# Rotary and convolution on the projections' banks, decays behind the rotary, and TensorE's side steps tied to products

## The chip, the cores and the metric

One core of a Trainium2 chip runs the whole program in one launch. The metric is the device time of that launch in microseconds (us). TensorE is PE (its weight load PEld), VectorE DVE, ScalarE ACT, GpSimd POOL; SyncE (SP) issues most loads.

## The reference, cut to what matters

Two layers of an encoder on 256 rows of 1024. Each layer projects the normalised rows, runs retention, a gated recurrence (LRU) and grouped-query attention on parts of the projection, adds the output projection, and then an expert stage (PEER). In float32:

```python
for l in range(DEPTH):                                   # 2
    h = rms_norm(x, ln1_w[l])
    rq, rk, rv, rg, lx, lgt, aq, ak, av = split_cols(h @ w_in[l], widths)
    o_ret = retention_group(rq, rk, rv, rg, ret_log_decay[l], ...)
    o_lru = rglru_group(lx, lgt, lru_conv_w[l], lru_conv_b[l], lru_gate_w[l], ...)
    o_att = attention_group(aq, ak, av, attn_q_norm[l], attn_k_norm[l], ax_cos, ax_sin)
    x = x + concat([o_ret, o_lru, o_att]) @ w_out[l]
    x = x + peer(rms_norm(x, ln2_w[l]), ...)
return rms_norm(x, lnf_w)

# attention: q, k normalised per head of 64, then rotary
qh = qh * cos + axial_rotate_half(qh) * sin              # the same for kh
o = softmax(qh @ kh.T * scale) @ vh
# LRU: 4-tap convolution along the rows (2 to the left, 1 to the right), two gates per direction, scan
xc = conv(xb, conv_w) + conv_b
# retention: scores times exp(log_decay * |i - j|)
scores = (q @ k.T) * dmat
```

## The kernel before, in words

Every product of two float32 matrices is made of three products of a high and a low half (`three`, L210). `split` (L144) makes the halves: ACT rounds `raw` to `hi`, and DVE or POOL subtracts to get `lo`. Weights arrive by SP in tiles `raw` (a ring of 4), `hi` and `lo` are rings of 4 as well, and nearly all splits of the mixing stage have their low half on POOL.

The mixing stage (`mix`, L249) runs once per layer, in these steps:

- Norm and transposes of the rows, in two blocks of 128 (`norm_rows` L175, `norm_T` L196).
- The attention's projection (`matt` L317): sums in three PSUM banks of the ring `acc` (4 banks), two for q and one for k and v of both blocks. Banks are copied to `qk` and `vt` (L344 to L346).
- The convolution's projection (L447 to L459): 4 weight tiles of 24 products each into both banks of the ring `hd`, called `pl`. `pl[0]` is copied into the padded tile `xpad` (L462), `pl[1]` into `gb`.
- The retention's projection (L529 to L540): 8 weight tiles of 12 products each into all four `acc` banks.
- The output projection (L611 on), then the expert stage (`peer`).

Beside the products runs side work, written as generators and advanced by a queue `Side` (L88): after a weight tile, `side.adv(us)` lets as many steps through as the given us pay for. The steps: `att` (L351: squares, `srq` = the power of the norm on POOL, rotary into `ro`, k scaled into `k2`, transposes to `qT` and `kT`; then scores, exponentials and the weighted sum), `lru` (L465: convolution, gates, scan), `decays` (L293: the retention's `dec`) and later `ret`. In layer 0 `setup` (L222) makes constants of the LRU by a chain of tiny DVE instructions.

What order instructions have on an engine is set by a scheduler that takes the ready instruction by its own estimates; `tc.issue_after(i)` adds the edge that what is written inside stands behind `i` on its engine. Each engine then runs its list in order. The scores take two `hd` banks at a time, `pe`; the gates take `hd` banks too.

Of the kernel before, what the change touches and what calls it, by code (L numbers as in the profile page):

```python
# [9 lines left out]
F32 = mybir.dt.float32  # L10
# [3 lines left out]
AF = mybir.ActivationFunctionType  # L14
# [4 lines left out]
P = 128  # L19
# [95 lines left out]
def trunk(ctx, tc, x, rows, lru_col, lru_gw, w_in, w_out, ln2_w, peer_wq, peer_kt, peer_ut, peer_v, lnf_w,  # L115
# [56 lines left out]
            st.enter_context(tc.issue_after(i))  # L172
        return st

    def norm_rows(wrow, tt, xn, add=None):  # L175

        st = sp.tile([P, 3], F32, tag="nst", bufs=4, name="nst")
        sq = sp.tile([P, 512], F16, tag="junk", bufs=1, name="junk")
        hs = [slice(hf * 512, (hf + 1) * 512) for hf in range(2)]
        for hf, o in enumerate(hs):  # L180
            if add is not None:
                V.tensor_add(xs[:, tt, o], xs[:, tt, o], add[hf])
            A.activation(sq, xs[:, tt, o], AF.Square, scale=1.0 / 32, accum_out=st[:, hf:hf + 1])
        with tc.issue_after(seen[0]) if tt else ExitStack():
            V.tensor_mul(xn[:, hs[0]], xs[:, tt, hs[0]], wrow[:, hs[0]])
        sm = V.tensor_scalar(st[:, 2:3], st[:, 0:1], st[:, 1:2], EPS, op0=ADD, op1=ADD)
        rs = sp.tile([P, 1], F32, tag="nrs", bufs=4, name="nrs")
        mark(G.tensor_tensor(rs, st[:, 2:3], mhalf[:, :1], op=POW))
        seen[0] = sm.ins
        with tc.issue_after(sm.ins):  # L190
            V.tensor_mul(xn[:, hs[1]], xs[:, tt, hs[1]], wrow[:, hs[1]])
        for o in hs:
            V.tensor_scalar(xn[:, o], xn[:, o], rs, None, op0=MUL)
            yield o

    def norm_T(wb, hiT, loT, tt, add=None, xn=None):  # L196
        if xn is None:
            xn = raw_tile()
        for o in norm_rows(wb, tt, xn, add):
            pt = tr_tile()  # L200
            for k in range(4):
                c = o.start + k * P
                TE.transpose(pt[:, k * P:(k + 1) * P], xn[:, c:c + P], ident)
            pv = pt.rearrange("p (k t) -> p k t", k=4)
            c = o.start // P
            o3 = (slice(None), slice(c, c + 4), slice(tt * P, (tt + 1) * P))
            mark(A.activation(hiT[o3], pv, AF.Copy))
            mark(V.tensor_sub(loT[o3], pv, hiT[o3].bitcast(F32)))

    def three(o, lh, ll, rh, rl, first, last, skip=False):  # L210
        TE.matmul(o, lh, rh, start=first, stop=False, skip_group_check=skip)  # L211
        TE.matmul(o, lh, rl, start=False, stop=False, skip_group_check=skip)  # L212
        TE.matmul(o, ll, rh, start=False, stop=last, skip_group_check=skip)  # L213

    hT = cp.tile([P, ND, T], F32R, name="hT")
    lT = cp.tile([P, ND, T], F32R, name="lT")
# [32 lines left out]
    def mix(l, mp, ms):  # L249
# [43 lines left out]
        def decays():  # L293
            V.tensor_scalar(gnw, gnw, 0.5, None, op0=MUL)

            for h in range(RH):
                tmp = ms.tile([P, NT, T], F32, tag="dtmp", bufs=1, name="dtmp")
                fw, bw = lg[:, h:h + 1], lg[:, RH + h:RH + h + 1]
                V.tensor_scalar(tmp, mnt[:, 1], bw, None, op0=MUL)
                V.scalar_tensor_tensor(tmp, mnt[:, 0], fw, tmp, op0=MUL, op1=ADD)  # L300
                A.activation(dec[:, h], tmp, AF.Exp)
                yield 1.2
# [34 lines left out]
        for d in range(HL, ND):  # L337
            watt(d)
            for tt in range(NT):
                matt(d, tt)  # L340
        qk = mp.tile([P, NT, 10, HD], F32, name="qk")
        vt = mp.tile([P, NT, P], F32, name="vt")
        for tt in range(NT):
            A.activation(qk[:, tt, 0:8], pq[tt].rearrange("p (h e) -> p h e", e=HD), AF.Copy)  # L344
            A.activation(qk[:, tt, 8:10], pkv[:, tt * T:tt * T + 128].rearrange("p (h e) -> p h e", e=HD), AF.Copy)
            V.tensor_copy(vt[:, tt], pkv[:, tt * T + 128:(tt + 1) * T])  # L346
        qT = mp.tile([P, 4, T], F32, name="qT")
        kT = mp.tile([P, 2, T], F32, name="kT")
        srq = mp.tile([P, NT, 10], F32, name="srq")

        def att():  # L351
            for tt in range(NT):
                sqt = ms.tile([P, 10, HD], F32, tag="art", name="asq")
                A.activation(sqt, qk[:, tt], AF.Square)
                ss = ms.tile([P, 10], F32, tag="ass", name="ass")
                V.tensor_reduce(ss, sqt, axis=AX.X, op=ADD)
                V.tensor_scalar(ss, ss, 1.0 / HD, EPS, op0=MUL, op1=ADD)
                G.tensor_tensor(srq[:, tt], ss, mhalf[:, :10], op=POW)
                ro = ms.tile([P, 10, HD], F32, tag="aro", name="aro")
                rt = ms.tile([P, 10, HD], F32, tag="art", name="art")  # L360
                for a, b, w in ((0, 8, 0), (8, 10, 1)):
                    V.tensor_mul(ro[:, a:b], qk[:, tt, a:b],
                                 acw[:, tt, w].unsqueeze(1).to_broadcast([P, b - a, HD]))
                    x5 = qk[:, tt, a:b].rearrange("p h (r s e) -> p h r s e", r=2, s=2)
                    r5 = rt[:, a:b].rearrange("p h (r s e) -> p h r s e", r=2, s=2)
                    s5 = asw[:, tt, w].rearrange("p (r s e) -> p r s e", r=2, s=2)
                    for s in range(2):
                        V.tensor_mul(r5[:, :, :, s], x5[:, :, :, 1 - s],
                                     s5[:, :, s].unsqueeze(1).to_broadcast([P, b - a, 2, 16]))
                V.tensor_add(ro, ro, rt)  # L370

                k2 = ms.tile([P, 2, 2, HD], F32, tag="k2", name="k2")
                for g in range(2):
                    A.activation(k2[:, g], ro[:, 8 + g].unsqueeze(1).to_broadcast([P, 2, HD]), AF.Copy,
                                 scale=srq[:, tt, 8 + g:9 + g])
                V.tensor_scalar(srq[:, tt], srq[:, tt], HD ** -0.5, None, op0=MUL)
                t = slice(tt * P, (tt + 1) * P)
                pt = tr_tile()
                for c in range(4):
                    TE.transpose(pt[:, c * P:(c + 1) * P], ro[:, 2 * c:2 * c + 2].rearrange("p h e -> p (h e)"), ident)  # L380
                V.tensor_copy(qT[:, :, t], pt.rearrange("p (c t) -> p c t", c=4))
                pt = tr_tile()
                for c in range(2):
                    TE.transpose(pt[:, c * P:(c + 1) * P], k2[:, c].rearrange("p o e -> p (o e)"), ident)
                A.activation(kT[:, :, t], pt[:, :2 * P].rearrange("p (c t) -> p c t", c=2), AF.Copy)
                yield 5.0
# [23 lines left out]
            for tt in range(NT):  # L410
# [24 lines left out]
                split(pt.rearrange("p (c t) -> p c t", c=4), mixH[:, 4:8, t], mixL[:, 4:8, t])  # L435
                yield 1.2

        side.add(att())
        side.adv(5.0)


        xpad = mp.tile([P, 2, T + 4], F32, name="xpad")
        gb = mp.tile([P, 2, T], F32, name="gb")
        V.memset(xpad, 0.0)
        if l == 0:
            setup()
        pl = [hd_tile() for _ in range(2)]  # L447
        for d2 in range(ND // 2):
# [5 lines left out]
            for k in range(2):  # L454
                d = d2 * 2 + k
                for c in range(4):
                    s = slice(k * 512 + c * P, k * 512 + (c + 1) * P)
                    three(pl[c // 2][:, (c % 2) * T:(c % 2 + 1) * T], hi[:, s], lo[:, s], hT[:, d], lT[:, d],
                          d == 0 and c % 2 == 0, d == ND - 1, skip=True)  # L459
# [70 lines left out]
        for d in range(ND):  # L530
# [4 lines left out]
            for tt in range(NT):  # L535
                t = slice(tt * P, (tt + 1) * P)
                for hf in range(2):
                    o = slice(hf * 512, (hf + 1) * 512)
                    three(pr4[tt][hf], hT[:, d, t], lT[:, d, t], hi[:, o], lo[:, o], d == 0, d == ND - 1)
# [435 lines left out]
```

## Time and profile before

| | |
|---|---|
| median of 3 runs | 1975.03 us (1974.86 to 1975.09) |
| the profiled execution, and its span | 1972.67 us, 1970.9 us |
| busy: PE, PEld | 1881.8 us (95%), 1671.8 us (85%) |
| busy: DVE, ACT, POOL | 1509.9 us (77%), 902.9 us (46%), 553.0 us (28%) |
| loaded | 321.16 MB, 163 GB/s over the span |

Layer 0's mixing stage takes about the first 165 us, layer 1's that from about 985 to 1140 us; the rest is the expert stage. In the page's table of 40 slices PE is at 9 tenths nearly everywhere else, and at 5 to 8 in these two stretches. PE's share is an average over both kinds of stages, so what a change in the mixing stage is worth has to be read there.

### The profile page before, as it was taken

How to read it: one execution, taken by the hardware profiler on the slowest of the kernel's cores; microseconds unless marked ns; L12 is line 12 of the kernel's file. 1: busy time of each engine (PE TensorE's matmuls, PEld its weight loads, DVE VectorE, ACT ScalarE, POOL GpSimd, SP SyncE). 2: the span in 40 equal slices, each digit the busy share in tenths (PEclk: the TensorE clock that was granted, in tenths of full speed). 3: DMA queues.
4: the chain of work that ended last, by engine and by line, in shares of the span. 5: the costliest groups of instructions: out<-in, count | busy, mean ns of one | idle time of the engine just before them, and what ended most of it. 6: DMA issues, size and time to landing. Idle time of an engine off the chain costs nothing.

```text
span 1970.9 us, 34224 instructions
## 1 busy us (share of the span) xinstructions
PE 1881.8 (95%) x13452; PEld 1671.8 (85%) x13452; DVE 1509.9 (77%) x2660; ACT 902.9 (46%) x1384; POOL 553.0 (28%) x240
## 2 busy tenths in 40 slices
PE   5888999999999999999978889999999999999998
PEld 5678999999999877788866689999999998777886
DVE  7676999789855699755576669996997557996555
ACT  4544444444444443444445344445444444334443
POOL 5425888200000132100073268881000002330000
PEclk9899999999999999999988999999999999999999
DMA  6225555544455544555552255555445555446553
GB/s 210 81 66 190 162 183 187 190 159 161 162 187 186 172 144 157 185 189 190 168 160 75 70 198 172 184 188 188 151 160 171 191 183 170 140 151 201 185 190 129
DMA packets 95138, 324.43 MB, mean 165 GB/s; under 512 B 10112, under 2 KB 10624, under 8 KB 94720
## 3 DMA queue, kind: packets, MB, share of 16 engines
q1 hardware_dynamic: 92672, 315.66, 48.8%
q10 hardware_dynamic: 2304, 6.59, 1.0%
q8 instruction: 105, 1.72, 0.4%
q14 instruction: 57, 0.47, 0.1%
HBM read 321.16 MB, written 1.05 MB: 163 GB/s over the span
## 4 chain that ended last, share of the span: by engine, by line
PE 77%; DVE 13%; issue 4%; POOL 3%; ACT 1%; DMA 1%; POOLq 0%; SPq 0%; DVEq 0%; ACTq 0%
PE acc L212 12%; PE acc L213 12%; PE acc L211 12%; PE hd L211 6%; PE hd L212 6%; PE hd L213 6%; PE tr L211 6%; PE tr L212 6%; PE tr L213 6%; DVE ob L791 2%; POOL lo L146 2%; DVE oa L794 2%; DVE Gt L806 1%; DVE pl L146 1%; DVE lo L146 1%
## 5 line engine op out<-in xcount | busy, mean ns | idle before, releaser
L145 ACT ACTIVATE hi<-raw 128x1024 fp32r<-128x1024 f32 (+1 forms) x600 | 627.9, 1047 | 507.1 <-issue 176.8
L146 POOL TENSOR_TENSOR lo<-raw,hi 128x1024 fp32r<-128x1024 f32 (+1 forms) x206 | 527.0, 2564 | 1175.0 <-ACT hi L145 1134.9
L146 DVE TENSOR_TENSOR lo<-raw,hi 128x1024 fp32r<-128x1024 f32 (+1 forms) x394 | 485.2, 1233 | 197.2 <-ACT hi L145 197.2
L211 PE MATMUL acc<-hi,ph 128*128 128x512 f32 x1024 | 410.7, 401 | 0.0
L213 PE MATMUL acc<-hi,pl 128*128 128x512 f32 x1024 | 405.3, 396 | 0.4 <-DVE pl L146 0.4
L212 PE MATMUL acc<-lo,ph 128*128 128x512 f32 x1024 | 405.4, 396 | 0.0
L211 PE MATMUL hd<-hT,hi 128*128 128x256 f32 x1088 | 311.2, 286 | 0.6 <-ACT hi L145 0.6
L213 PE MATMUL hd<-hT,lo 128*128 128x256 f32 x1088 | 308.3, 283 | 2.2 <-POOL lo L146 2.2
L212 PE MATMUL hd<-lT,hi 128*128 128x256 f32 x1088 | 308.0, 283 | 0.0
L211 PE MATMUL tr<-hT,hi 128*128 128x256 f32 x1024 | 291.2, 284 | 0.0
L145 ACT ACTIVATE ph<-Gt 128x256 fp32r<-128x256 f32 x256 | 106.4, 417 | 401.9 <-PE acc L212 392.1
L212 PE MATMUL tr<-lT,hi 128*128 128x256 f32 x1024 | 288.1, 281 | 0.0
L213 PE MATMUL tr<-hT,lo 128*128 128x256 f32 x1024 | 287.9, 281 | 0.0
L213 PEld LDWEIGHTS acc<-hi,pl 128*128 128x128 f32 x1024 | 192.9, 188 | 47.3 <-DVE pl L146 2.0
L212 PEld LDWEIGHTS acc<-lo,ph 128*128 128x128 f32 x1024 | 193.3, 189 | 41.1
L211 PEld LDWEIGHTS acc<-hi,ph 128*128 128x128 f32 x1024 | 193.1, 189 | 40.8 <-ACT ph L145 0.5
L146 DVE TENSOR_TENSOR pl<-Gt,ph 128x256 fp32r<-128x256 f32 x256 | 123.2, 483 | 126.9 <-ACT ph L145 126.9
L213 PEld LDWEIGHTS hd<-hT,lo 128*128 128x128 f32 x1088 | 207.3, 191 | 2.6 <-POOL lo L146 2.6
L211 PEld LDWEIGHTS hd<-hT,hi 128*128 128x128 f32 x1088 | 207.6, 191 | 2.2 <-ACT hi L145 0.8
L212 PEld LDWEIGHTS hd<-lT,hi 128*128 128x128 f32 x1088 | 207.3, 191 | 0.9
L211 PEld LDWEIGHTS tr<-hT,hi 128*128 128x128 f32 x1024 | 193.4, 189 | 1.1
L212 PEld LDWEIGHTS tr<-lT,hi 128*128 128x128 f32 x1024 | 193.3, 189 | 1.0
(206 smaller groups left out, 2536.5 us busy)
## 6 DMA issues: line engine op xcount, KB each, us to landing
raw<-in_peer_ut_dram SPq DMA_DIRECT2D x256, 512.0 KB, 3.4
raw<-in_peer_v_dram SPq DMA_DIRECT2D x256, 512.0 KB, 3.6
raw<-in_peer_wq_dram SPq DMA_DIRECT2D x32, 512.0 KB, 4.2
raw<-in_w_in_dram SPq DMA_DIRECT2D x24, 512.0 KB, 3.7
raw<-in_w_out_dram SPq DMA_DIRECT2D x16, 512.0 KB, 3.4
raw<-in_w_in_dram SPq DMA_DIRECT2D x16, 384.0 KB, 4.0
Gt<-in_peer_kt_dram ACTq DMA_DIRECT2D x2, 1024.0 KB, 4.7
xs<-in_x_dram SPq DMA_DIRECT2D x2, 512.0 KB, 6.0
```

What stands on the lines that cost most here:

```text
L145: A.activation(hi, src, AF.Copy)
L146: (lo_eng or V).tensor_sub(lo, src, hi.bitcast(F32))
L211: TE.matmul(o, lh, rh, start=first, stop=False, skip_group_check=skip)
L212: TE.matmul(o, lh, rl, start=False, stop=False, skip_group_check=skip)
L213: TE.matmul(o, ll, rh, start=False, stop=last, skip_group_check=skip)
L791: V.tensor_tensor(four(ob), iop(0, P), pair(1, P), op=EQ)
L794: V.tensor_mul(four(oa[:, z]), four(oe), pair(2 + z, SW))
L806: V.scalar_tensor_tensor(g, pv[:, o:o + n], 1.0 / GS, g, op0=MUL, op1=MUL)
```

## The change

- `norm_rows` and `norm_T` can give the last scaling of the first half of a row block to ACT; the mixing stage's two norms do so.
- The copies `qk` and `xpad` are gone. Squares, rotary products and convolution read the `acc` and `hd` banks; the convolution's taps are cut at the ends in place of padding. `vt` is copied by ACT.
- `att` makes the rotary of both blocks first, then the transposes of both; `decays` is tied on DVE behind the last rotary sum.
- The gates' products go to a `tr` bank in place of an `hd` bank.
- The side steps during the last two tiles of the convolution's projection, and all during the retention's, are tied behind the last product before them (`side_adv`).

```diff
-    def norm_rows(wrow, tt, xn, add=None):
+    def norm_rows(wrow, tt, xn, add=None, act=False):
...
-        for o in hs:
-            V.tensor_scalar(xn[:, o], xn[:, o], rs, None, op0=MUL)
+        for hf, o in enumerate(hs):
+            if act and hf == 0:
+                A.activation(xn[:, o], xn[:, o], AF.Copy, scale=rs)
+            else:
+                V.tensor_scalar(xn[:, o], xn[:, o], rs, None, op0=MUL)
...
-                V.tensor_scalar(tmp, mnt[:, 1], bw, None, op0=MUL)
+                with tc.issue_after(last[0].ins):
+                    V.tensor_scalar(tmp, mnt[:, 1], bw, None, op0=MUL)
...
-        qk = mp.tile([P, NT, 10, HD], F32, name="qk")
-        for tt in range(NT):
-            A.activation(qk[:, tt, 0:8], pq[tt].rearrange("p (h e) -> p h e", e=HD), AF.Copy)
-            A.activation(qk[:, tt, 8:10], pkv[:, tt * T:tt * T + 128].rearrange("p (h e) -> p h e", e=HD), AF.Copy)
-            V.tensor_copy(vt[:, tt], pkv[:, tt * T + 128:(tt + 1) * T])
...
+                qp = pq[tt].rearrange("p (h e) -> p h e", e=HD)
+                kp = pkv[:, tt * T:tt * T + 128].rearrange("p (h e) -> p h e", e=HD)
-                A.activation(sqt, qk[:, tt], AF.Square)
+                A.activation(sqt[:, 0:8], qp, AF.Square)
+                A.activation(sqt[:, 8:10], kp, AF.Square)
...
-                V.tensor_add(ro, ro, rt)
+                A.activation(vt[:, tt], pkv[:, tt * T + 128:(tt + 1) * T], AF.Copy)
+                last[0] = V.tensor_add(ro, ro, rt)
...
+                turned.append((ro, k2))
+                yield 5.0
+            for tt in range(NT):
+                ro, k2 = turned[tt]
...
         side.add(att())
-        side.adv(5.0)
-        xpad = mp.tile([P, 2, T + 4], F32, name="xpad")
+        side.adv(10.0)
+        def side_adv(us):
+            with tc.issue_after(lastp[0].ins):
+                side.adv(us)
...
-            if d2 == 1:
-                side.adv(5.0)
-        A.activation(xpad[:, :, 2:2 + T], pl[0].rearrange("p (c t) -> p c t", c=2), AF.Copy)
+            if d2 >= 2:
+                side_adv(5.0)
...
-                V.tensor_scalar(xc[:, ct], xpad[:, ct, 0:T], w(0), w(4), op0=MUL, op1=ADD)
-                for j in range(1, 4):
-                    V.scalar_tensor_tensor(xc[:, ct], xpad[:, ct, j:j + T], w(j), xc[:, ct], op0=MUL, op1=ADD)
+                px = pl[0][:, ct * T:(ct + 1) * T]
+                V.tensor_scalar(xc[:, ct], px, w(2), w(4), op0=MUL, op1=ADD)
+                for j, a, b in ((0, 2, T), (1, 1, T), (3, 0, T - 1)):
+                    V.scalar_tensor_tensor(xc[:, ct, a:b], px[:, a + j - 2:b + j - 2], w(j), xc[:, ct, a:b],
+                                           op0=MUL, op1=ADD)
...
-                    pg = hd_tile()
+                    pg = tr_tile()
...
-            side.adv(R_MIX)
+            side_adv(R_MIX)
```

How that moves instructions, at three places of layer 0 (L145 and L146 are `split`; the names are those of the code, and behind the arrow stands what is read).

PE, where the transposes of the rotary's block 0 stand among the products of the convolution's projection. Before:

```order
L213 MATMUL hd<-hT,lo 128x256
L211 MATMUL hd<-hT,hi 128x256
L212 MATMUL hd<-lT,hi 128x256
L380 MATMUL tr<-ident,aro 128x128 x4
L384 MATMUL tr<-ident,k_334 128x128
L213 MATMUL hd<-hT,lo 128x256
L384 MATMUL tr<-ident,k_334 128x128
L211 MATMUL hd<-hT,hi 128x256
```

and after:

```order
L215 MATMUL hd<-hT,hi 128x256
L216 MATMUL hd<-lT,hi 128x256
L217 MATMUL hd<-hT,lo 128x256
L389 MATMUL tr<-ident,aro 128x128 x4
L393 MATMUL tr<-ident,k_329 128x128 x2
L215 MATMUL hd<-hT,hi 128x256
L216 MATMUL hd<-lT,hi 128x256
```

Before, 38 of the 96 products stand ahead of them, after 72; those of block 1 then stand behind all 96 (60 before).

ACT, from the high halves of the attention's last weight tiles (128x768) to the first reads of the `acc` banks. Before:

```order
L235 ACTIVATE lt_358<-lt_357 128x8
L145 ACTIVATE hi<-raw 128x768 x2
L301 ACTIVATE dec<-dtmp 128x512
L145 ACTIVATE hi<-raw 128x768 x2
L301 ACTIVATE dec<-dtmp 128x512
L145 ACTIVATE hi<-raw 128x1024
L301 ACTIVATE dec<-dtmp 128x512
L145 ACTIVATE hi<-raw 128x1024
L301 ACTIVATE dec<-dtmp 128x512
L145 ACTIVATE hi<-raw 128x1024
L344 ACTIVATE qk<-acc 128x512 x2
```

and after:

```order
L145 ACTIVATE hi<-raw 128x768 x3
L239 ACTIVATE lt_362<-lt_361 128x8
L145 ACTIVATE hi<-raw 128x768
L145 ACTIVATE hi<-raw 128x1024 x3
L358 ACTIVATE asq<-acc 128x512
L359 ACTIVATE asq<-acc 128x128
L145 ACTIVATE hi<-raw 128x1024
L358 ACTIVATE asq<-acc 128x512
L374 ACTIVATE vt<-acc 128x128
```

The exponentials of the decays are gone from between the high halves; `setup`'s exponential (`lt`, L235 before, L239 after) has moved behind three of them.

DVE, from the rotary's last sum to the reduces of the first scores. Before:

```order
L370 TENSOR_TENSOR aro<-aro,art 128x640
L381 COPY qT<-tr 128x4x128
L376 TENSOR_SCALAR srq<-srq 128x10
L469 TENSOR_SCALAR xc<-xpad,pcol 128x256 x2
L471 SCALAR_TENSOR_TENSOR xc<-xpad,pcol,xc 128x256 x6
L515 TENSOR_SCALAR gu<-gu 128x512
L516 TENSOR_TENSOR gu<-gu,gb 128x512
L399 TENSOR_REDUCE sm<-hd 128x2 x2
```

and after, the middle of the same stretch:

```order
L390 COPY qT<-tr 128x4x128
L485 SCALAR_TENSOR_TENSOR xc<-hd,pcol,xc 128x254
L485 SCALAR_TENSOR_TENSOR xc<-hd,pcol,xc 128x255
L304 TENSOR_SCALAR dtmp<-mnt,prm 128x512
L485 SCALAR_TENSOR_TENSOR xc<-hd,pcol,xc 128x255
L483 TENSOR_SCALAR xc<-hd,pcol 128x256
L305 SCALAR_TENSOR_TENSOR dtmp<-mnt,prm,dtmp 128x512
L485 SCALAR_TENSOR_TENSOR xc<-hd,pcol,xc 128x254
L408 TENSOR_REDUCE sm<-hd 128x2
L485 SCALAR_TENSOR_TENSOR xc<-hd,pcol,xc 128x255
L410 SCALAR_TENSOR_TENSOR sm<-sm,srq 128x2
```

The decays' instructions (L304, L305) now lie among the convolution's, and the first reduce stands ahead of the convolution's end.

## Rows read from the trace of the kernel before

**Rows 1.** the page's chain that ended last, shares of the span by engine
```profile
PE 77%; DVE 13%; issue 4%; POOL 3%; ACT 1%; DMA 1%; POOLq 0%; SPq 0%; DVEq 0%; ACTq 0%
```

**Rows 2.** PE timeline, layer 0: start, length, line, shapes [idle before, releaser], us
```profile
35.90 0.28 PE L211 MATMUL hd<-hT,hi 128*128 128x256 f32 x1
...
51.06 1.09 PE L380 MATMUL tr<-ident,aro 128*128 128x128 f32 x4 [6.08 <-DVE aro L370]
...
62.26 0.40 PE L211 MATMUL acc<-hi,hT 128*128 128x512 f32 x1
...
94.71 0.60 PE L417 MATMUL tr<-ident,pr 128*128 128x128 f32 x4
```

**Rows 3.** PE timeline, layer 1, the same columns
```profile
1014.12 0.28 PE L211 MATMUL hd<-hT,hi 128*128 128x256 f32 x1
...
1014.24 0.28 PE L212 MATMUL hd<-lT,hi 128*128 128x256 f32 x1
...
1026.27 1.08 PE L380 MATMUL tr<-ident,aro 128*128 128x128 f32 x4 [7.05 <-DVE aro L370]
...
1037.46 0.39 PE L211 MATMUL acc<-hi,hT 128*128 128x512 f32 x1
...
1070.12 0.60 PE L417 MATMUL tr<-ident,pr 128*128 128x128 f32 x4
```

**Rows 4.** POOL timeline, layer 0
```profile
39.50 7.58 POOL L146 TENSOR_TENSOR lo<-raw,hi 128x1024 fp32r<-128x1024 f32 x3 [3.71 <-ACT hi L145]
...
49.91 2.08 POOL L358 TENSOR_TENSOR srq<-ass,mhalf 128x10 f32<-128x10 f32 x1 [2.84 <-DVE ass L357]
...
130.92 2.35 POOL L146 TENSOR_TENSOR lo<-raw,hi 128x1024 fp32r<-128x1024 f32 x1 [4.64 <-ACT hi L145]
```

**Rows 5.** DVE timeline, layer 0
```profile
33.47 2.35 DVE L243 TENSOR_SCALAR lt<-lt 128x8 f32<-128x8 f32 x1
...
35.85 0.17 DVE L242 TENSOR_TENSOR lt<-lt,lt 128x8 f32<-128x8 f32 x1
...
36.05 0.17 DVE L243 TENSOR_SCALAR lt<-lt 128x8 f32<-128x8 f32 x1
...
41.98 5.65 DVE L362 TENSOR_TENSOR aro<-qk,acw 128x512 f32<-128x512 f32 x2 [2.19 <-ACT qk L344]
...
63.48 6.72 DVE L471 SCALAR_TENSOR_TENSOR xc<-xpad,pcol,xc 128x256 f32<-128x256 f32 x6
...
71.18 1.28 DVE L399 TENSOR_REDUCE sm<-hd 128x2 f32<-128x512 f32 x2
...
130.36 1.28 DVE L574 SCALAR_TENSOR_TENSOR dec<-hd,dec 128x512 f32<-128x512 f32 x2
```

**Rows 6.** ACT timeline, layer 0
```profile
37.84 0.63 ACT L301 ACTIVATE dec<-dtmp 128x512 f32<-128x512 f32 x1 [4.53 <-DVE dtmp L300]
...
47.86 0.28 ACT L345 ACTIVATE qk<-acc 128x128 f32<-128x128 f32 x1 [4.38 <-DVE vt L346]
...
74.27 0.56 ACT L405 ACTIVATE pr<-hd,sm,srq 128x256 f32<-128x256 f32 x1
```

**Rows 7.** DVE timeline, layer 1
```profile
988.90 3.97 DVE L193 TENSOR_SCALAR pr<-pr,nrs 128x512 f32<-128x512 f32 x2
...
1000.76 0.48 DVE L299 TENSOR_SCALAR dtmp<-mnt,prm 128x512 f32<-128x512 f32 x1
...
1001.27 0.75 DVE L300 SCALAR_TENSOR_TENSOR dtmp<-mnt,prm,dtmp 128x512 f32<-128x512 f32 x1
```

**Rows 8.** DVE groups by shape, 0 to 165 us: names, shapes, count | busy us, mean ns | idle
```profile
L356 DVE TENSOR_REDUCE ass<-asq 128x10 f32<-128x640 f32 x2 | 1.6, 809 | 0.0
...
L597 DVE TENSOR_TENSOR rsq<-gg,rss 128x256 f32<-128x256 f32 x2 | 0.8, 420 | 0.8 <-POOL rss L594 0.8
...
L596 DVE TENSOR_TENSOR gg<-hd,gg 128x256 f32<-128x256 f32 x2 | 0.8, 417 | 0.0
```

More of the change, by code (lines that the diff above doesn't have):

```diff
@@ L191, in norm_rows @@
             V.tensor_mul(xn[:, hs[1]], xs[:, tt, hs[1]], wrow[:, hs[1]])
-        for o in hs:
-            V.tensor_scalar(xn[:, o], xn[:, o], rs, None, op0=MUL)
+        for hf, o in enumerate(hs):
[3 more added lines that the diff above has]
+                V.tensor_scalar(xn[:, o], xn[:, o], rs, None, op0=MUL)
             yield o
     def norm_T(wb, hiT, loT, tt, add=None, xn=None):
+        act = xn is not None
         if xn is None:
             xn = raw_tile()
-        for o in norm_rows(wb, tt, xn, add):
+        for o in norm_rows(wb, tt, xn, add, act):
             pt = tr_tile()
@@ L212, in three @@
         TE.matmul(o, lh, rl, start=False, stop=False, skip_group_check=skip)
-        TE.matmul(o, ll, rh, start=False, stop=last, skip_group_check=skip)
+        return TE.matmul(o, ll, rh, start=False, stop=last, skip_group_check=skip)
     hT = cp.tile([P, ND, T], F32R, name="hT")
@@ L351, in att @@
         def att():
+            turned = []
             for tt in range(NT):
+                qp = pq[tt].rearrange("p (h e) -> p h e", e=HD)
+                kp = pkv[:, tt * T:tt * T + 128].rearrange("p (h e) -> p h e", e=HD)
                 sqt = ms.tile([P, 10, HD], F32, tag="art", name="asq")
-                A.activation(sqt, qk[:, tt], AF.Square)
+                A.activation(sqt[:, 0:8], qp, AF.Square)
+                A.activation(sqt[:, 8:10], kp, AF.Square)
                 ss = ms.tile([P, 10], F32, tag="ass", name="ass")
@@ L360, in att @@
                 rt = ms.tile([P, 10, HD], F32, tag="art", name="art")
[L361 to L364, printed above, removed]
+                for a, b, w, src in ((0, 8, 0, qp), (8, 10, 1, kp)):
+                    V.tensor_mul(ro[:, a:b], src, acw[:, tt, w].unsqueeze(1).to_broadcast([P, b - a, HD]))
+                    x5 = src.rearrange("p h (r s e) -> p h r s e", r=2, s=2)
                     r5 = rt[:, a:b].rearrange("p h (r s e) -> p h r s e", r=2, s=2)
@@ L436, in att @@
                 yield 1.2
+        last = [None]
         side.add(att())
-        side.adv(5.0)
-        xpad = mp.tile([P, 2, T + 4], F32, name="xpad")
+        side.adv(10.0)
+        def side_adv(us):
+            with tc.issue_after(lastp[0].ins):
+                side.adv(us)
         gb = mp.tile([P, 2, T], F32, name="gb")
-        V.memset(xpad, 0.0)
         if l == 0:
@@ L457, in mix @@
                     s = slice(k * 512 + c * P, k * 512 + (c + 1) * P)
-                    three(pl[c // 2][:, (c % 2) * T:(c % 2 + 1) * T], hi[:, s], lo[:, s], hT[:, d], lT[:, d],
-                          d == 0 and c % 2 == 0, d == ND - 1, skip=True)
-            if d2 == 1:
-                side.adv(5.0)
-        A.activation(xpad[:, :, 2:2 + T], pl[0].rearrange("p (c t) -> p c t", c=2), AF.Copy)
+                    lastp = [three(pl[c // 2][:, (c % 2) * T:(c % 2 + 1) * T], hi[:, s], lo[:, s], hT[:, d], lT[:, d],
+                                   d == 0 and c % 2 == 0, d == ND - 1, skip=True)]
+            if d2 >= 2:
+                side_adv(5.0)
         A.activation(gb, pl[1].rearrange("p (c t) -> p c t", c=2), AF.Copy)
@@ L538, in mix @@
                     o = slice(hf * 512, (hf + 1) * 512)
-                    three(pr4[tt][hf], hT[:, d, t], lT[:, d, t], hi[:, o], lo[:, o], d == 0, d == ND - 1)
-            side.adv(R_MIX)
+                    lastp = [three(pr4[tt][hf], hT[:, d, t], lT[:, d, t], hi[:, o], lo[:, o], d == 0, d == ND - 1)]
+            side_adv(R_MIX)
         rqk = mp.tile([P, NT, 8, HD], F32, name="rqk")
```

## The prediction

> **What bounds the kernel now.** I read the chain of waits on the page first: TensorE (PE) carries 77% of it [rows 1], so only time in which PE stands still can be won. Nearly all of the span is the expert stage, which the change leaves as it is. It touches the mixing stage, run once per layer, and there I followed PE's own list of instructions. In layer 0 the first product of the convolution's projection (96 products into the hd banks) starts at 35.90, the first product of the retention projection at 62.26 and the first transpose of softmax weights at 94.71 [rows 2]; in layer 1 the same marks are 1014.12, 1037.46 and 1070.12 [rows 3]. So 96 products, 0.12 us apart [rows 3] and worth 11.5 us, take 26.4 and 23.3 us. The reader is to see why: PE stands 6.08 us in layer 0 and 7.05 us in layer 1 for aro, the rotary's sum [rows 2, 3].
>
> Behind both stands one thing. A VectorE (DVE) instruction on SBUF data that meets a split on GpSimd (POOL) ends only when the split ends: an eight-column instruction took 2.35 us where its like takes 0.17, and the rotary's first two products 5.65 us, while POOL ran splits back to back from 39.50 to 47.08 [rows 4, 5]. The decays (four times two DVE instructions and an exponential on ScalarE, ACT) sit in front of the rotary. ACT stood 4.53 us for one of them [rows 6] with the next split's high half queued behind it, and so POOL stood 3.71 us [rows 4]. The copies out of the banks wait too: one copy of k stood 4.38 us for DVE's copy of v [rows 6]. DVE on a bank is not held up so: two instructions with a PSUM operand took 1.28 us together beside a split that ran from 130.92 to 133.27 [rows 4, 5].
>
> **The change part by part.** I count per layer against these marks, in the time of the profiled execution, 1972.67 us (its span 1970.9 and 1.8 around it). The median of the runs is 2.4 us above that, which I add at the end.
>
> *Norm.* One half of each normalised row goes to ACT. In layer 1 the two halves on DVE took 3.97 us together behind two splits [rows 7]; the half that stays waits for one split at most and ACT's half for none, so the first transposes come some 2 us sooner: -2. In layer 0 there is no such stretch, and the load of the LRU's parameters now stands behind the norm on ACT's queue. I take -0.5, between 0 and -2.
>
> *From the convolution's projection to the retention products.* Gone are ACT's copies of q and k and its copy into xpad, a memset, and from DVE the copies of v (now ACT's). None is on PE's path once the rotary doesn't wait for them: 0. The square, the rotary's products and the convolution read the banks. That could be dearer per instruction, but the same 128x256 shape takes 417 ns with an operand in a bank and 420 ns from SBUF alone [rows 8]: 0 again. [...]
>
> With the decays gone from the front, ACT gives out high halves as data comes, and POOL's own queue sets the pace: three splits after the one that the first products need, the power for block 0 (srq), one split, the power for block 1. A split is 2.35 us and a power 2.08 [rows 4]: 4 x 2.35 + 2 x 2.08 = 13.6 us after the projection's start. ACT's k2 and two transposes are 1.2 more (k2's like, the exponential, is 0.56 [rows 6]). PE meanwhile does 72 products (8.6 us), block 0's transposes and 24 products (2.9 us), and is not later. 14.8 us in place of 23.3 in layer 1: -8.5.
>
> In layer 0 a chain of 21 tiny DVE instructions, setup(), is ahead of the rotary in DVE's queue. By the order its exponential now comes behind three high halves on ACT, so the chain falls among POOL's splits and gets one instruction through per split: about 8 by the end of the last. Then POOL has nothing before the rotary's sum of squares, and the other 13 go at 0.2 us each [rows 5], 2.6 us. Block 0's rotary as far as srq costs a 128x512 product (0.64), two 128x256 (0.83) and the reduce (0.81) [rows 5, 8], 2.3 us. That puts everything behind the third split 4.9 us later: 14.8 + 4.9 = 19.7 in place of 26.4, -6.7. If the chain passes unhindered it is as in layer 1, 26.4 - 14.8 = 11.6 saved.
>
> *From there to the first transpose of softmax weights.* 48 products lie between these marks, before as after, in 32.5 us. Two things move against each other. Against: DVE had the convolution (its six updates 6.72 us) and gelu before the scores' reduce at 71.18, 8.9 us after the first product [rows 2, 5]. Now the convolution is 8 x 0.42 = 3.4 [rows 8], but the decays, 4 x (0.48 + 0.75) = 4.9 [rows 7], lie among it, and I let four of their instructions meet a split of 2.35 us. The convolution also holds the bank that the second half of the first score group needs, and ACT's copies of k's transposes stand behind the decays' exponentials, so PE waits twice for some 4 us. The second reduce comes some 16 us after the first product: +7. For: the LRU's gates go to the tr banks. Before, they shared the two hd banks with the scores, and from the first score groups' last exponential, 74.83, to 94.71 it took 19.9 us [rows 2, 6]. What ACT has to do in it is twelve exponentials at 0.56 [rows 6] and twelve activations of the gates of the same width, some 13 us: -7. The loss is in the queues and sure; the gain needs everything to fit, so I count 4 of it: +3 per layer, with ends 0 and +7.
>
> *After that* DVE and PE do the same work in nearly the same order: 0.
>
> Sum: layer 0 -0.5 - 6.7 + 3 = -4.2; layer 1 -2 - 8.5 + 3 = -7.5. Together -11.7: 1961.0 in the profiled execution's time, **1963.4 us** as a median.
>
> **Rivals.**
> 1. *Given back behind the decays.* If the gates' own banks win nothing, the third term is +7 in both layers: -0.2 and -3.5, 1971.3 us. For it: the scores were late before, with DVE's queue full [rows 5], and that queue gets fuller. Against it: scores and gates visibly take turns on two banks.
> 2. *Slower: the scores start too late.* One mechanism decides. The eight decay instructions, and the three small ones on SBUF among them, can each end with a split of its own. Four meetings are in the sum; each further one costs 2.35 us, since PE's products are tied behind the scores and can't go ahead. The saving of 11.7 us is used up with 5 further meetings, two and a half per layer. With eight meetings per layer it is 8 x 2.35 - 11.7 = 7 us slower, 1982 us. Against it: ACT's high halves stand behind the decays' exponentials, so POOL runs dry and leaves DVE alone.
> 3. *All of it holds.* The gates' banks bring the whole 7 and the setup chain slips through between the splits: -1.5, -11.6 and 0 in layer 0, -2, -8.5 and 0 in layer 1. That is -23.6, 1951.4 us.
> 4. *The stall is not moved.* The tensor add that ends the rotary still reads SBUF and can wait for a split, and with it PE. If PE's 6.08 and 7.05 us stay, the second terms shrink to about -1 and -1.5, and 1976 us is left, no change that could be told.
>
> **How the numbers follow.** The forecast gets 0.60, case 1 0.15, case 4 0.06, case 2 0.10 and case 3 0.09. A measurement of this kernel can tell about 0.2%, 4 us, from no change. Faster by more than that: the forecast, case 3 and a third of case 1, 0.74. Within 0.2% (1971.1 to 1979.0): the rest of case 1, case 4 and a little of case 2, 0.17. Slower: 0.09. The range reaches from 1951 (case 3) to 1975 (case 1 with one or two more meetings) and leaves out about 0.15.
>
> **What would show it.** PE's wait for aro falls to under 5 us in layer 0 and under 2 in layer 1. The first retention product comes 20 us after the first hd product in layer 0 and 15 in layer 1. Between it and the first softmax transposes PE waits for the scores' inputs twice, some 4 us each, for ACT (gb, k's transposes) and for DVE (the convolution); the rotary's 128x512 product takes some 0.7 us, not 2.8. The second term is wrong if POOL shows gaps between the projection's splits; the third if the softmax transposes come over 37 us or under 31 us after the first retention product.

## The result and the profile after

The changed kernel takes **1961.19 us** (median of 4 runs, 1956.96 to 1963.86) against 1974.94 us of the kernel before in the same comparison: ratio 0.9936, 95% interval 0.9925 to 0.9948. It is faster by 0.64%; 1963.4 us was predicted, with a range of 1951 to 1975. The profiled execution took 1961.07 us, its span is 1959.3.

The page's busy times and its chain that ended last (answers to [rows 1]):

```profile
PE 1879.7 (96%) x13452; PEld 1671.3 (85%) x13452; DVE 1491.7 (76%) x2650; ACT 904.3 (46%) x1386; POOL 565.0 (29%) x240
PE 78%; DVE 16%; issue 3%; ACT 1%; POOL 1%; DMA 1%; POOLq 0%; SPq 0%; DVEq 0%; ACTq 0%
```

TensorE's list in layer 0 (start, length, line, shapes [idle before, releaser]; answers to [rows 2]; line numbers are 4 to 15 higher than before):

```profile
35.39 0.28 PE L215 MATMUL hd<-hT,hi 128*128 128x256 f32 x1
...
48.28 1.09 PE L389 MATMUL tr<-ident,aro 128*128 128x128 f32 x4 [4.21 <-DVE aro L375]
...
57.58 0.67 PE L389 MATMUL tr<-ident,aro 128*128 128x128 f32 x4 [4.24 <-DVE qT L390]
...
58.33 0.78 PE L215 MATMUL acc<-hi,hT 128*128 128x512 f32 x1
...
70.92 1.30 PE L403 MATMUL hd<-kT,qT 64*128 64x256 f32 x4 [4.05 <-DVE xc L485]
...
90.74 0.60 PE L426 MATMUL tr<-ident,pr 128*128 128x128 f32 x4
...
129.26 2.38 PE L600 MATMUL hd<-rv,dec 128*128 128x64 f32 x12 [0.19 <-DVE dec L589]
...
131.97 4.36 PE L600 MATMUL hd<-rv,dec 128*128 128x64 f32 x20
...
138.79 0.63 PE L615 MATMUL tr<-ident,rsq 128*128 128x128 f32 x2
```

And in layer 1 (answers to [rows 3]):

```profile
1011.40 0.28 PE L215 MATMUL hd<-hT,hi 128*128 128x256 f32 x1
...
1019.92 0.60 PE L389 MATMUL tr<-ident,aro 128*128 128x128 f32 x4
...
1027.87 1.11 PE L389 MATMUL tr<-ident,aro 128*128 128x128 f32 x4 [4.14 <-DVE qT L390]
...
1029.06 0.78 PE L215 MATMUL acc<-hi,hT 128*128 128x512 f32 x1
...
1039.92 1.13 PE L403 MATMUL hd<-kT,qT 64*128 64x256 f32 x4 [2.50 <-DVE xc L485]
...
1060.64 0.60 PE L426 MATMUL tr<-ident,pr 128*128 128x128 f32 x4
...
1100.84 2.34 PE L600 MATMUL hd<-rv,dec 128*128 128x64 f32 x20
...
1104.46 0.42 PE L615 MATMUL tr<-ident,rsq 128*128 128x128 f32 x2
```

The wait of 7.05 us for the rotary's sum is gone in layer 1, and that of layer 0 is 4.21 instead of 6.08. In the place of the old waits stand new ones: 4.24 and 4.14 us for the copy `qT`, which must empty a tr bank before block 1 can be transposed, and 4.05 and 2.50 us for the convolution. VectorE's list in layer 0 shows why `qT` is late; GpSimd's power for block 1 and its next split stand above it:

```profile
50.92 2.00 POOL L363 TENSOR_TENSOR srq<-ass,mhalf 128x10 f32<-128x10 f32 x1 [0.18 <-DVE ass L362]
52.85 2.34 POOL L146 TENSOR_TENSOR lo<-raw,hi 128x1024 fp32r<-128x1024 f32 x1
```

```profile
52.92 2.82 DVE L305 SCALAR_TENSOR_TENSOR dtmp<-mnt,prm,dtmp 128x512 f32<-128x512 f32 x1
...
56.44 0.48 DVE L304 TENSOR_SCALAR dtmp<-mnt,prm 128x512 f32<-128x512 f32 x1 [0.62 <-ACT dec L306]
56.84 0.68 DVE L390 COPY qT<-tr 128x512 f32<-128x512 f32 x1
```

A decay instruction (0.75 us where nothing meets it, [rows 7]) ended at 55.74, 0.55 us behind the split that ran from 52.85 to 55.19, and a second decay instruction, which waited for the first one's exponential, stood ahead of the copy.

Layer 0 was 3.97 us ahead at its first softmax transposes (90.74 for 94.71) and 0.48 us *behind* at the retention's (138.79 against 138.31 in the kernel before, the line below). Its waits between these marks are 4.1 us together, 3.9 before.

```profile
138.31 0.42 PE L600 MATMUL tr<-ident,rsq 128*128 128x128 f32 x2
```

But TensorE ran at half its clock there (granted 0.50). The windows view of the stretch, before and then after (busy us of PE, PEld, DVE, ACT and POOL, then the granted clock, DMA share, GB/s):

```profile
130.00:140.00 10.00, 9.06 (x56) 7.13 (x57) 5.49 (x14) 2.85 (x5) 4.36 (x3) 1.00 0.33 104
```

```profile
130.00:140.00 10.00, 10.00 (x39) 9.10 (x39) 3.09 (x9) 2.21 (x4) 2.02 (x2) 0.50 0.00 0
```

The 20 products of line 600 took 4.36 us in layer 0, at half clock, and 2.34 in layer 1, at full clock. At the end of layer 0 the changed kernel is 1.5 us ahead, and layer 1 adds 10.1.

### The profile page after: what moved, and what is told of

Read it like the earlier page. It is cut to its first block, busy times and chain, and to the rows that moved or that the text cites. A ratio compares the mean times of both kernels' runs of the same rounds, so it can differ in the third digit from the quotient of the medians.

```text
span 1959.3 us, 34218 instructions
## 1 busy us (share of the span) xinstructions
PE 1879.7 (96%) x13452; PEld 1671.3 (85%) x13452; DVE 1491.7 (76%) x2650; ACT 904.3 (46%) x1386; POOL 565.0 (29%) x240
## 4 chain that ended last, share of the span: by engine, by line
PE 78%; DVE 16%; issue 3%; ACT 1%; POOL 1%; DMA 1%; POOLq 0%; SPq 0%; DVEq 0%; ACTq 0%
PE acc L216 12%; PE acc L217 12%; PE acc L215 12%; PE hd L215 6%; PE tr L215 6%; PE hd L216 6%; PE hd L217 6%; PE tr L216 6%; PE tr L217 6%; DVE ob L806 2%; DVE oa L809 2%; DVE Gt L821 2%; DVE lo L146 2%; DVE pl L146 2%; PE hd L816 1%
## 5 line engine op out<-in xcount | busy, mean ns | idle before, releaser
L146 POOL TENSOR_TENSOR lo<-raw,hi 128x1024 fp32r<-128x1024 f32 (+1 forms) x206 | 539.9, 2629 | 1151.6 <-ACT hi L145 1112.7
L145 ACT ACTIVATE hi<-raw 128x1024 fp32r<-128x1024 f32 (+1 forms) x600 | 629.9, 1050 | 509.1 <-issue 176.6
L146 DVE TENSOR_TENSOR lo<-raw,hi 128x1024 fp32r<-128x1024 f32 (+1 forms) x394 | 489.9, 1244 | 199.8 <-ACT hi L145 199.5
L145 ACT ACTIVATE ph<-Gt 128x256 fp32r<-128x256 f32 x256 | 106.9, 419 | 400.0 <-PE acc L216 390.8
L146 DVE TENSOR_TENSOR pl<-Gt,ph 128x256 fp32r<-128x256 f32 x256 | 124.9, 490 | 127.0 <-ACT ph L145 127.0
```

Of the source, the lines that this page charges most:

```text
L145: A.activation(hi, src, AF.Copy)
L146: (lo_eng or V).tensor_sub(lo, src, hi.bitcast(F32))
```

## The experiments

Twelve kernels ran, most of them the changed kernel with one edit. "Clock" is the mean granted clock over the timed executions, and it matters: within one kernel (the rotary on SBUF, below) single executions went from 1960.0 us at 0.986 to 1975.4 at 0.976. A least-squares line through all 118 executions, one level per kernel and one common slope, gives 1.26 us (plus or minus 0.16, 95%) per 0.001 of clock. The last column is each kernel's level at 0.983 by that line; it is a reading, not a measurement.

It may take too much away from an edit. In the traces of all these kernels the half clock lies in the mixing stages, where the edits act: 0.87 to 0.97 was granted there (0 to 165 and 975 to 1145 us), 0.99 or 1.00 in the expert stages. And in the changed kernel's first trace TensorE fell to half clock at the end of each of the five long waits shown above (4.21, 4.24 and 4.05 us in layer 0, 4.14 and 2.50 in layer 1) or within 1.3 us behind it, for 3 to 10 us each time. An edit that removes a wait may thus raise the clock too, and the column then counts that part of its worth as clock. So read the median as the edit's whole effect, with the chance of the clock in it, and the column as a cautious level.

| kernel | median us | ratio, 95% interval | clock | at 0.983 |
|---|---|---|---|---|
| before (46 runs) | 1972.4 to 1974.4 | 1 | 0.9813 | 1971.3 |
| changed, again | 1960.8 | 0.992 to 0.995 | 0.9830 | 1960.7 |
| decays untied | 1959.8 | 0.991 to 0.995 | 0.9845 | 1961.7 |
| rotary on SBUF | 1966.9 | 0.995 to 0.998 | 0.9812 | 1964.9 |
| both of these | 1962.9 | 0.992 to 0.995 | 0.9838 | 1966.4 |
| convolution on SBUF | 1965.0 | 0.993 to 0.997 | 0.9823 | 1963.8 |
| gates on hd | 1969.4 | 0.998 to 1.000 | 0.9803 | 1967.4 |
| no ties | 1960.4 | 0.991 to 0.994 | 0.9830 | 1960.1 |
| norm on VectorE | 1955.5 | 0.989 to 0.993 | 0.9865 | 1959.3 |
| before + gates on tr | 1972.6 | 0.998 to 1.000 | 0.9799 | 1967.2 |
| decays behind convolution | 1952.6 | 0.987 to 0.991 | 0.9857 | 1955.2 |
| norm + decays | 1948.2 | 0.986 to 0.990 | 0.9870 | 1953.5 |
| norm + decays + setup | 1947.1 | 0.985 to 0.989 | 0.9875 | 1953.2 |

**The changed kernel again**

> The changed kernel once more, beside the others of this group. Theory: 1961 us, within 3. In the first trace TensorE ran at half clock from 129 to 139 us of layer 0, where the kernel before had the full clock, and that gave back the 4 us that layer 0 had won by its first transpose of softmax weights. If that stretch belongs to the order of the work, it comes again at the same place and the transposes of the retention's output (line 615) come at 138.8 again. If it is a matter of one execution, they come near 134.5 and that execution is some 4 us shorter.

1960.8 us. In layer 0 every mark came within 0.12 us of the first trace, half clock from 129 to 140 included, so there the first reading holds. In layer 1 the marks did not come again: half clock stood at 1041 to 1052 in the first trace, and at 1095 to 1106 in this one, which won 4.6 us ahead of the softmax transposes (26.95 us from the first retention product against 31.58) and lost 3.9 behind them (47.74 to the retention's transposes against 43.82). So the stretch isn't fixed to one instruction, and what a layer gains in one place can be taken back in another.

**The decays untied**

```diff
-                with tc.issue_after(last[0].ins):
-                    V.tensor_scalar(tmp, mnt[:, 1], bw, None, op0=MUL)
+                V.tensor_scalar(tmp, mnt[:, 1], bw, None, op0=MUL)
```

> The decays lose their place behind the rotary (the tie is taken off, the rest of the change stays); the order of instructions then puts all eight decay instructions of VectorE ahead of the rotary's first product again, in both layers. Theory A (the decays' place is what mattered): the time from the first product of the convolution's projection to the first retention product goes back from 22.9 and 17.7 us towards the 26.4 and 23.3 of the kernel before, TensorE's wait for the rotary's sum to 6 or 7 us in both layers, and the whole takes about 1970 us. Theory B (reading the banks is what mattered): TensorE's wait stays where the change has it, and the time within 3 us of 1961.

1959.8 us: theory A falls. With the decays in front, the waits for the rotary's sum were 1.39 us and none, not 6 or 7. VectorE in layer 1 shows why:

```profile
1003.00 2.21 DVE L304 SCALAR_TENSOR_TENSOR dtmp<-mnt,prm,dtmp 128x512 f32<-128x512 f32 x1
...
1014.19 0.69 DVE L366 TENSOR_TENSOR aro<-acc,acw 128x512 f32<-128x512 f32 x1 [2.20 <-ACT asq L357]
1014.80 0.41 DVE L371 TENSOR_TENSOR art<-acc,asw 128x256 f32<-128x256 f32 x1
```

The decays meet splits as before, but while TensorE is busy with the attention's projection; they are through 2.2 us before the rotary can start. The rotary then reads banks at 0.69 and 0.41 us an instruction. What the tie wins ahead of the first retention product (0.9 and 2.6 us) is not kept behind it.

**The rotary on SBUF copies**

```diff
+        for tt in range(NT):
+            A.activation(qk[:, tt, 0:8], pq[tt].rearrange(...), AF.Copy)
+            A.activation(qk[:, tt, 8:10], pkv[...].rearrange(...), AF.Copy)
+            V.tensor_copy(vt[:, tt], pkv[...])
...
-                qp = pq[tt].rearrange("p (h e) -> p h e", e=HD)
+                qp = qk[:, tt, 0:8]
```

> The rotary and its squares read copies of q, k and v in SBUF again (three copies per block, as before), with the decays still behind the rotary; the convolution still reads its bank. Theory A (the decays' place): the copies pass beside the splits and cost nothing on TensorE's path, 1961 us within 3. Theory B (the banks): the rotary's two wide products have SBUF operands alone again, each ends only with the split that it meets, 2.35 us, and block 0's rotary comes up to 4.7 us later in each layer: 1966 to 1970 us.

1966.9 us, theory B by the time. Its mechanism shows in layer 1: two products that take 0.41 us each on a bank took 5.15, while GpSimd ran splits back to back up to 1022.48:

```profile
1014.73 7.75 POOL L146 TENSOR_TENSOR lo<-raw,hi 128x1024 fp32r<-128x1024 f32 x3 [0.28 <-ACT hi L145]
```

```profile
1016.84 0.84 DVE L372 TENSOR_TENSOR aro<-qk,acw 128x512 f32<-128x512 f32 x1 [13.33 <-ACT qk L349]
1017.61 5.15 DVE L377 TENSOR_TENSOR art<-qk,asw 128x256 f32<-128x256 f32 x2
...
1026.62 0.41 DVE L377 TENSOR_TENSOR art<-qk,asw 128x256 f32<-128x256 f32 x1
```

In layer 0 it does not. There the chain of `setup()` held the rotary until the splits were over, and two such products took 0.75 us together. TensorE's waits in this stretch of layer 0 are 11.2 us together, 8.5 in the changed kernel: 4.89 for the sum, 1.08 for ScalarE's `k`, 1.70 for its `kT` and 3.57 for `qT`, the last again behind a decay instruction that had met a split:

```profile
44.70 0.75 DVE L377 TENSOR_TENSOR art<-qk,asw 128x256 f32<-128x256 f32 x2
...
57.66 2.64 DVE L304 TENSOR_SCALAR dtmp<-mnt,prm 128x512 f32<-128x512 f32 x1
```

```profile
61.74 0.69 PE L397 MATMUL tr<-ident,k 128*128 128x128 f32 x2 [3.57 <-DVE qT L394]
```

From the first hd product to the first retention product it took 26.9 and 21.1 us (22.9 and 17.7 in the changed kernel, 26.4 and 23.3 before). The profile is of its slowest execution, at 0.976, so its own marks are on the high side; the level at equal clock is 4 us above the changed kernel.

**Both undone**

> Both at once: the decays without their tie and the rotary on SBUF copies. Each alone had left most of the gain (medians 1959.8 and 1966.9 us against 1960.8 of the changed kernel and 1972.4 of the one before). Theory D (either is enough, since a stall needs both: the high halves and copies on ScalarE queued behind the decays, and rotary products that end only with a split): undoing both brings the wait for the rotary's sum back to 6 or 7 us in both layers, the stretch from the first hd product to the first softmax transposes to 56 us and more, and the time to 1969 to 1974 us. Theory E (the two add up): the losses are 0 and some 6 us, so 1965 to 1968 us.

By the marks theory D: 25.6 and 22.7 us, nearly what it was before, though with waits of 2.69 and 3.64 us in place of 6 or 7. By the time neither: 1962.9 us, from 1958.4 at a clock of 0.988 to 1974.4 at 0.979; the profiled execution took 1972.0. At equal clock the loss is 5.7 us, close to the 1.0 and 4.2 of the two alone, which speaks for E. The median alone can't tell it from the changed kernel.

The four kernels make a square. Us from the first hd product to the first retention product, layer 0 and layer 1, one trace each (so the clock is in them):

| | decays ahead of the rotary | decays behind it |
|---|---|---|
| rotary on SBUF copies | 25.6, 22.7 | 26.9, 21.1 |
| rotary on banks | 23.8, 20.3 | 22.9, 17.7 |

Reading the banks wins 1.8 to 3.9 us of a layer in either column; the decays' place wins between -1.3 and 2.6.

**The convolution on SBUF**

```diff
+        A.activation(xpad[:, :, 2:2 + T], pl[0].rearrange("p (c t) -> p c t", c=2), AF.Copy)
...
-                V.tensor_scalar(xc[:, ct], px, w(2), w(4), op0=MUL, op1=ADD)
+                V.tensor_scalar(xc[:, ct], xpad[:, ct, 0:T], w(0), w(4), op0=MUL, op1=ADD)
```

> The one part not yet tried alone: the convolution reads the padded copy xpad in SBUF again, all else as changed. Theory H (reading the bank is a gain): its eight instructions take longer wherever they meet a split (the six updates took 6.72 us before, 0.47 us each on the bank), the gates come later, and the time is 2 to 5 us more than the changed kernel's 1960.8. Theory I (reading the bank is a loss): TensorE's second score group waits 4.05 and 1.2 to 2.5 us for the convolution to give up the hd bank; with the copy the bank is free after ScalarE's copy of 0.6 us, those waits go, and the time is 2 to 5 us less.

1965.0 us, theory H. Its wait for the second score group went to ScalarE (3.20 and 3.63 us for exponentials) and the convolution met splits:

```profile
1034.80 2.62 DVE L485 TENSOR_SCALAR xc<-xpad,pcol 128x256 f32<-128x256 f32 x1
...
1038.34 2.57 DVE L485 TENSOR_SCALAR xc<-xpad,pcol 128x256 f32<-128x256 f32 x1
```

**The gates on hd, and on tr alone**

```diff
-                    pg = tr_tile()
+                    pg = hd_tile()
```

> The LRU's gates take hd banks again, in turns with the scores, all else as changed. The prediction counted 4 us per layer for the gates' own banks: the stretch from the first retention product to the first softmax transposes, 32.4 and 27 to 31.6 us in the changed kernel, would be 36 in both layers and the whole some 8 us longer, 1969 us. Rival: the scores wait for ScalarE's exponentials and not for the banks; within 3 us of 1961.

1969.4 us, as the prediction's term would have it, but not where it had put it: from the first retention product to the first softmax transposes it took 34.45 and 28.12 us, only 2.0 and 1.2 us more than in the changed kernel's second trace. The rest of the loss is spread over later places, and no line names one cause for it. Scores and gates take turns again (TensorE, layer 0):

```profile
87.41 1.03 PE L493 MATMUL hd<-xc,gwt 128*128 128x256 f32 x4
...
89.40 1.13 PE L493 MATMUL hd<-xc,gwt 128*128 128x256 f32 x4 [0.74 <-ACT pr L414]
90.47 1.13 PE L403 MATMUL hd<-kT,qT 64*128 64x256 f32 x4
```

The last scores come at 91.96 for 88.18. Of the 8.6 us, 6.7 are left at equal clock. The other way round, in the kernel before:

> The kernel before, with one line of the change: the LRU's gates take tr banks instead of hd banks. Putting them back on hd in the changed kernel had cost 8.6 us (1969.4 against 1960.8). Theory F (the gates' banks carry most of the gain by themselves): some 8 us faster than the kernel before, 1965 to 1967 us, with the stretch from the first retention product to the first softmax transposes 3 to 6 us shorter in each layer. Theory G (they only pay once the scores come as the changed kernel has them): within 3 us of the kernel before, 1971 to 1977 us.

1972.6 us against 1972.9: theory G by the time. The stretch is 1.1 and 1.4 us shorter, not 3 to 6. The second score group still waits 3.33 us in both layers for exponentials, and the wait for the rotary stays (9.76 and 7.04 us). Its clock was the lowest of all kernels; at equal clock it would be 4 us ahead, half of theory F's 8. By the times, what one line brings depends on what the others have cleared.

**Without the ties**

> The side steps without their ties to the projection's products, all else as changed. If the ties only fix an order that the scheduler takes anyway, 1961 us within 3 and the same order of products around the scores. If they matter, the scores or the transposes of the rotary stand earlier in TensorE's list and wait longer there: 2 to 6 us slower.

1960.4 us, and the same waits within 0.2 us of the changed kernel's second trace: the ties of the side steps do nothing here.

**The norm on VectorE**

```diff
-        act = xn is not None
+        act = False
```

> Both halves of the normalised rows on VectorE again, all else as changed. The first transposes of layer 1 come after 3.6 us of waiting instead of 2.1, so 1.5 to 2 us are lost there and about 0.5 in layer 0: 1963 us. Rival: the half on ScalarE holds up something else by as much, no difference, 1961 us.

1955.5 us: both theories fall, the ScalarE half costs 5 us by the medians (1.4 at equal clock). In layer 1 it is worth 1.5 us at the first transposes (2.10 for 3.58 us of waiting), of which the rest of the norm gives back 0.9. In layer 0 it moves two things on ScalarE: the load of the LRU's parameters, which is issued there 6.1 us later, and the exponential of the `setup()` chain. The changed kernel, and then this one:

```profile
18.89 0.33 ACTq L281 DMA_DIRECT2D pcol<-in_lru_col_dram  x1
...
24.04 0.85 ACT L145 ACTIVATE hi<-raw 128x768 fp32r<-128x768 f32 x1 [4.56 <-PE acc L217]
...
26.94 0.19 ACT L239 ACTIVATE lt<-lt 128x8 f32<-128x8 f32 x1
```

```profile
12.79 0.33 ACTq L281 DMA_DIRECT2D pcol<-in_lru_col_dram  x1
...
21.07 0.21 ACT L239 ACTIVATE lt<-lt 128x8 f32<-128x8 f32 x1 [1.72 <-DVE lt L238]
```

The load by itself delays little: the chain's first instruction on VectorE (L238) starts at 20.87 here and at 21.14 there. What counts is the exponential's place in ScalarE's list. Here it runs at once, at 21.07; there it stands behind three high halves, the first of which waits 4.56 us for TensorE, and comes at 26.94. Why the scheduler put it there, whether for the later load or for the norm itself, no run shows. Here 14 of the chain's 21 instructions behind the exponential are through by 25.08, at 0.16 to 0.20 us each (the other seven take 1.74 to 2.34 each), and the rotary starts at 39.29 in place of 44.19. The changed kernel, and this one:

```profile
44.19 0.69 DVE L367 TENSOR_TENSOR aro<-acc,acw 128x512 f32<-128x512 f32 x1
```

```profile
39.29 0.68 DVE L367 TENSOR_TENSOR aro<-acc,acw 128x512 f32<-128x512 f32 x1
```

TensorE's 4.21 us in layer 0 are gone (block 1 waits 5.25 for `qT`), and in this trace neither layer had half clock in the retention.

**The decays one step further back, and a faster kernel**

```diff
-                    V.scalar_tensor_tensor(xc[:, ct, a:b], ...)
+                    last[0] = V.scalar_tensor_tensor(xc[:, ct, a:b], ...)
                 yield 1.6
+            side.add(decays())
...
         side.add(lru())
-        side.add(decays())
```

> The decays go one step further back: tied behind the last update of the convolution instead of the rotary's sum. In the changed kernel TensorE waits 4.24 and 4.14 us for the transposes of the rotary's second block, since VectorE's copy of the first block's transposes (qT) stands behind a decay instruction that ended with a split (2.82 us), and 4.05 and 2.50 us for the convolution, with decays between its updates. Theory A: all four waits fall to under 1 us, 10 to 14 us in all, of which some is lost to whatever ends last then: 1947 to 1953 us. Theory C (the splits on GpSimd, or ScalarE's high halves, would be as late without the decays): the waits take another releaser and 1958 to 1963 us remain.

1952.6 us, theory A by the time. Of the four waits two fell under 1 us: that for block 1's transposes is 0.20 us in layer 0 and 2.55 in layer 1, now for ScalarE's copy `kT`, as theory C has it, and the convolution's is 2.71 and none. Nothing needs the decays before the retention's scores, at 125 us of layer 0 in the changed kernel. Together with the norm on VectorE:

> The changed kernel with the norm wholly on VectorE and the decays tied behind the convolution. Alone these gave 1955.5 and 1952.6 us, 5.3 and 8.3 less than the changed kernel. The first takes away layer 0's wait for the rotary's sum (4.2 us), the second the waits for block 1's transposes (4.2 us in each layer) and the convolution. They are different waits, so if they add up 1947 us, within 3; if what the one wins is waited for elsewhere, 1951 to 1954 us.

**1948.2 us**, ratio 0.9879 (0.9862 to 0.9896), as the sum said. TensorE in layer 0 waits for no score, and only once for more than half a microsecond between the first and the last of these marks:

```profile
36.53 0.28 PE L215 MATMUL hd<-hT,hi 128*128 128x256 f32 x1
...
45.05 0.60 PE L389 MATMUL tr<-ident,aro 128*128 128x128 f32 x4
...
51.40 0.66 PE L389 MATMUL tr<-ident,aro 128*128 128x128 f32 x4 [2.55 <-ACT kT L394]
...
52.60 0.48 PE L215 MATMUL acc<-hi,hT 128*128 128x512 f32 x1
...
78.44 0.60 PE L426 MATMUL tr<-ident,pr 128*128 128x128 f32 x4
```

16.1 and 25.8 us between the three marks, in place of 22.9 and 32.4. With the chain of `setup()` behind the convolution too:

> The same with the chain of tiny instructions of setup() tied behind the convolution as well. With the norm on VectorE the chain is through before the rotary in layer 0, so moving it takes no wait away: 1947 us like its neighbour, within 3. If it stands between the scores' reduces there, each of its instructions that meets a split holds the scores up by 2.3 us: 2 to 5 us slower than its neighbour.

1947.1 us, the same within what can be told; one score waits 1.68 us for a chain instruction.

## Why the prediction was right, and where its steps failed

The sum of -11.7 us met -11.6 in the profiled execution, but by terms that missed in both directions: layer 0 gave 1.5 us of the 4.2 predicted, layer 1 10.1 of 7.5. That the sum agrees to 0.1 us is luck; that it got faster, with most of the gain ahead of the retention's products, is not.

- **Norm.** -0.5 in layer 0, as said. In layer 1 -1.2, not -2: the first hd product came 2.72 us sooner, 1.52 of which were layer 0's. The prediction saw the exponential come behind three high halves and charged the price (+4.9) to the next term, without tying it to an edit. The run with the norm on VectorE shows that it is the norm's own, and by the medians it makes the edit a loss.
- **To the retention's products.** -3.4 and -5.7 measured, -6.7 and -8.5 predicted. The step that failed is "PE meanwhile does ... and is not later": it forgot that block 1's transposes need a tr bank which VectorE empties, and that the decays now stand ahead of that copy. What it counted for GpSimd came: the second power ended 17.5 and 12.9 us after the first hd product, 18.5 and 13.6 predicted. With the decays behind the convolution the stretch took 20.8 and 16.6 us, near the 19.7 and 14.8 of the prediction.
- **Its cause.** The prediction gave this gain to the decays and put the reading of banks at 0. The square of four kernels shows the banks ahead: they win 1.8 to 3.9 us of a layer with the decays in either place, the decays' place -1.3 to 2.6. How the banks win is shown where products on SBUF meet splits: in layer 1 with the decays behind, and in both layers with the decays ahead (in the kernel before two 128x512 products took 5.65 us in layer 0 and 3.48 in layer 1; with the rotary on SBUF one that met no split took 0.68). In layer 0 with the decays behind they met none, and why the banks win there is open. The rows were there: 5.65 us for the two products that read SBUF, and the bank operands that weren't held up [rows 4, 5]. The working even used the bank's durations, but called the edit free.
- **To the softmax transposes.** 0.0 and -1.1 measured, +3 predicted. The convolution's wait came (4.05 and 2.50); the one for ScalarE (`gb`, k's transposes) did not. The gates' banks are worth 8.6 us by the medians, as counted, but only 3.2 of it in the two stretches. In the second trace layer 1's stretch is 26.95 us, under the 31 at which the prediction wanted the term called wrong; the half clock had left that stretch.
- **After that, 0.** +4.5 in layer 0 by the retention's transposes, and that is the clock (layer 1 has the same six waits there, 4.1 us, and took 43.8 us at full clock for 48.1); 2.0 of it came back later, half of that in the expert stage. -2.1 in layer 1.

Of the rivals, the first falls with the 8.6 us that the gates' banks are worth, and the third needed -11.6 where layer 0 gave -3.4. The second named a mechanism that is real (decay instructions that meet splits: 2.82, 1.82, 2.43 and 2.52 us in layer 0, four as counted), with a price paid in an earlier place. The fourth was wrong: the add at the rotary's end took 0.82 us and waited for no split. Of the marks, the waits for the sum and the product of 0.69 us came as said; 20 and 15 us did not.

What stays open is what sets the half clock. In layer 0 of the changed kernel TensorE had waited 0.96, 0.69 and 0.77 us in the ten microseconds before it fell at 129; in layer 1 of the same trace it had the same three waits, from 1089 to 1097, and did not fall. In the kernel before it had waited 2.02 us there in layer 0 and did not fall, 2.00 in layer 1 and did. No row tells the one from the other, and no run held the clock fixed. That some 10.6 us of the gain are work (the levels at equal clock) and the rest clock is an estimate, and too low for the work if the waits that went had lowered the clock.

## What to carry to other kernels

Where VectorE works beside GpSimd, count for each of its instructions whether all operands lie in SBUF: here those that met a split ended only behind it (5.15 us for two products of 0.41), and the bank that the data came from was the better source. When work is moved back, look for the last place ahead of its first use, not for the nearest free one: behind the rotary the decays won nothing in the whole time, behind the convolution 8 us by the medians. An edit on one engine can also move what else is in its list: half a norm on ScalarE put a 0.2 us exponential 5.9 us back, and the rotary with it. And where single executions differ by more than an edit brings, look at the granted clock, but do not take it for something apart from the edit.

## What the runs showed of the hardware

- The clock weighs as much as the change: between executions of one kernel 15.3 us went with 0.010 of mean granted clock, and in two executions of the changed kernel layer 1's long half-clock stretch stood in two places (1041 to 1052, 1095 to 1106).
- GpSimd's power didn't hold VectorE up as its splits do: the rotary's add, with all operands in SBUF, took 0.82 us while the power ran (changed kernel, layer 0).

```profile
46.43 1.96 POOL L363 TENSOR_TENSOR srq<-ass,mhalf 128x10 f32<-128x10 f32 x1 [3.60 <-DVE ass L362]
```

```profile
47.31 0.82 DVE L375 TENSOR_TENSOR aro<-aro,art 128x640 f32<-128x640 f32 x1
```

- Away from splits, reading a bank took about as long as reading SBUF: the rotary's 128x256 product 0.41 us from a bank and 0.41 from SBUF, the convolution's updates 0.47 us from either. Only the first instruction of each convolution differed: 0.53 us on the bank, two in 0.72 on SBUF.
